# Seams between the stages of a fused eight-core decoder layer: an input load moved, normalisation work respread over the engines, output writes moved into the next pass

## Chip, cores and metric

The kernel is one SPMD program on all eight cores of one Trainium2 chip (two dies of four cores). The time is the device time of the slowest core, in microseconds (us). Engines: PE (TensorE, matmuls), DVE (VectorE), ACT (ScalarE), POOL (GpSimd, which also issues the weight loads here), SP (SyncE). An execution of all eight cores has a second, slower state, in which the cores of a die show a lower clock: in the changed kernel's run of 1408.84 us, cores 0 to 3 show 0.812 to 0.822 and the other four 0.989 or 0.990.

## The reference, cut to what matters

```python
def layer(h, p, ...):
    xn = rmsnorm(h); z = xn @ w_in                    # mixer A: short conv; mixer B: chunked gMLP
    ...
    h = h + m @ w_o
    up = rmsnorm(h) @ w_up                            # up-projection, then causal dwconv
    ...
    h = h + (jax.nn.gelu(fa) * fb) @ w_down           # down-projection
    gate = jax.nn.sigmoid(rmsnorm(h, g_ple) @ w_ple_gate)
    h = h + gate * (p @ w_ple)                        # per-layer embedding
y = rmsnorm(h, g_final)
```

There are 8 prompts of 2048 positions and 128 samples of one position, model width 1024, feed-forward width 2816. Each core takes one prompt and 16 samples.

## The kernel before

Activations lie channels first: 8 tiles of 128 channels, positions along the free axis. A core makes two passes of 1024 positions (pass 0 has its 16 samples too), each in three blocks of 384, 384 and 256 (272) positions. One pass is: first projection (v), conv stage (the head of it is seam A in pass 0 and seam D in pass 1), spatial stage, merge, output projection, up-projection (its start is seam B), down-projection, embedding stage (seam C in pass 0, seam E in pass 1). A list of operations per engine is built in program order, and semaphores are put in from the reads and writes, so **the order in which the Python code appends operations is the order in which each engine executes them**. That order is what the change is about. For example, on core 1 of the kernel before, POOL stood idle for 6.82 us, halved the embedding input (5.47 us) and issued the weight loads that stand behind it at 89.80 us.

A norm has four parts: squares on ACT, their sum over the 8 channel tiles on DVE or POOL, one matmul with ones that sums over the partitions (PE) and an Ln and an Exp on ACT, then 8 products. In the last stage of pass 1 (`self.pe`) PE sums the squares itself, with one small matmul for each tile into a held bank.

```python
class Norm:
    def _emit(self, k, b, late=False):
        ...
        if self.pe:                         # L444: square on ACT; L446: matmul with ones into the held bank
            if q == 0: self.bank[bi] = psR.get(hold=True)
            P.op("act", ... Square ...)
            P.op("pe", ... matmul(pt[:, 0:N], lhsT=ones[:], rhs=out, start=(q == 0), stop=(q == 7)) ...)
            return
        P.op("act", ... Square ...)                                         # L460
        ...
        P.op(self.eng, ... tensor_tensor(dst, acc, out, op=ALU.add) ...)     # L469, on POOL or DVE

    def rstd(self, b):
        self.flush(bi)
        pt, ptr = self.bank.get(bi) or psR.get()
        if bi in self.bank: psR.held.discard(ptr[1])        # the held bank goes back into rotation here
        else: group(pt[:, 0:N], [ones x ssb, ones x sqb])   # the statistics matmuls on PE
        P.op("act", ... Ln ...); P.op("act", ... Exp ...)   # L490, L491

    def to_xn(self, b, gi, spread=False):   # L501: 8 DVE products per block, input of the next projection
    def to_y(self, b, gi, parts, spread=False):  # L515: 8 DVE products in place, then stores
```

`bg` is a queue of such products: `spread=True` leaves them there, and `bg_run(n)` appends n of them between other work.

```python
def load_pT(p):                             # embedding input
    load(pT..., pt_d[p]..., eng="pool")
    P.op("pool", ... tensor_scalar(pT, pT, 0.5, op0=ALU.mult))              # L576
# called in pass 0 after setup_state(), in pass 1 after the first projection; that is, ahead of the conv stage

# start of the up-projection
for c in range(3):
    g_part(c, [b0])
    if c == 1: nrm.to_xn(b2, 1, True)
    else: bg_run(4)
for b in (b1, b2):
    for c in range(3):
        g_part(c, [b]); bg_run(4)
        ...

# embedding stage
fn = Norm(p, "pool", delay=2)
fn.pe = p == 1
for b in blocks:
    for i in range(8):
        fn.step()
        pG, pGr = psR.get(); pE, pEr = psR.get()
        proj(pG, ...); group(pE[:, 0:N], ...)                 # 8 + 2 matmuls
        ... tanh (ACT, L1015), gate (DVE, L1016), add (POOL or DVE, L1019) ...
        fn.add(i, b)
        bg_run(...)
        if bi == 0 and i == 0: nrm.to_xn(b1, 2, True)
        if bi == 0 and i == 7: nrm.to_xn(b2, 2, True)
        if bi > 0 and i == 1 and not (p == 0 and bi == 2): fn.to_y(blocks[bi - 1], 3, 2, True)
```

`psR` hands out the eight PSUM banks in rotation and skips held ones.

## Time and profile before

| kernel before | value |
|---|---|
| median of the four runs given first | 1260.41 us: two fast (1227.80, 1233.55), two slow (1287.27, 1289.82) |
| with the runs beside the changed kernel, 16 runs | median 1229.27 us |
| profiled run | span 1232.0 us on core 1 |

The median lies between two states. The spans of single cores in the profiled execution before show one more thing to note: the slowest core is 8.7 us above the median of the eight (1223.35, the mean of the fourth and fifth).

```profile
core 1: 1232.0 us, clock 0.977
...
core 7: 1218.1 us, clock 0.984
die 0 (median of its cores): 1225.0 us, clock 0.982
die 1 (median of its cores): 1222.3 us, clock 0.983
```

The dies agree, so the state is fast, and core 1 lost its excess by itself. One operation's statistics (count, then shortest, median and longest duration in ns) show a second thing, which isn't particular to core 1. It is the scaling of a tile of v on DVE:

```profile
L640 DVE TENSOR_SCALAR s_R<-s_R,s_rv x16: 475/478/5648, 79.6 to 707.7; 128x1024 bf16<-128x1024 bf16 x16
```

The same work took 0.48 us and, once, 5.65 us. The prediction takes the rest of the profile apart.

### The profile page before, as it was taken

To read this page: it belongs to the slowest core of one execution; us is meant where nothing else is said; L and a number is where in the kernel's file an instruction comes from. 1 tells how busy PE (TensorE), PEld (TensorE's weight loads), DVE (VectorE), ACT (ScalarE), POOL (GpSimd) and SP (SyncE) were. 2 spreads that over 40 slices of the span, in tenths; PEclk is the share of its full clock that TensorE was granted. 3 is DMA by queue.
4 is the path that set the end of the run, shared out by engine and by line. 5 is a ranking of instruction groups with operands and counts; after the bars stand their busy time and mean duration, and the time that the engine had idled before them with its cause. 6 is when DMAs were issued, how large, how long until landed. Compare 5 with 4: busy or idle time off the path is not lost.

```text
span 1232.0 us, 24272 instructions; the slowest of 8 cores (1218.1 to 1232.0 us)
## 1 busy us (share of the span) xinstructions
PE 1154.9 (94%) x7870; PEld 764.8 (62%) x7870; DVE 718.7 (58%) x1338; ACT 510.7 (41%) x1036; POOL 374.8 (30%) x411
## 2 busy tenths in 40 slices
PE   3898999999989999999889899999998999999975
PEld 2574666666656666666467566666665666666643
DVE  3346675222588999546663766522258899951266
ACT  3652232212446655343748133311134655541264
POOL 0140101222315343265560210122231534333241
PEclk9898999999999999999889899999999999999998
DMA  7737453333335332563349636333333533135303
GB/s 185 158 32 125 86 89 52 69 70 69 69 69 104 70 69 49 170 120 70 69 125 217 174 72 118 53 70 69 69 70 69 104 70 70 28 70 103 72 7 137
DMA packets 36234, 109.67 MB, mean 89 GB/s; under 512 B 10224, under 2 KB 10736, under 8 KB 35984
## 3 DMA queue, kind: packets, MB, share of 16 engines
q0 software_dynamic: 22016, 82.86, 37.6%
q1 hardware_dynamic: 14096, 25.27, 6.6%
q8 instruction: 67, 1.10, 0.3%
q14 instruction: 55, 0.45, 0.1%
HBM read 181.01 MB, written 9.95 MB: 155 GB/s over the span
## 4 chain that ended last, share of the span: by engine, by line
PE 79%; DVE 7%; ACT 6%; issue 4%; DMA 3%; POOL 1%; DVEq 0%; SPq 0%; POOLq 0%; ACTq 0%
PE pq L381 67%; PE pq L924 11%; DVE s_xn L501 3%; DMA s_ring<-win 2%; DMA s_h<-xt 1%; DVE s_h L515 1%; ACT L490 1%; ACT s_wide L613 1%; ACT s_rsb L490 1%; ACT s_R L606 1%; ACT L1015 1%; PE pq L679 1%; DVE s_R L640 1%; DVE s_wide L1016 1%; DVE s_h L819 1%
## 5 line engine op out<-in xcount | busy, mean ns | idle before, releaser
L381 PE MATMUL pq<-s_xn,s_ring 128*128 128x386 bf16 (+5 forms) x5184 | 801.6, 312 | 22.8 <-DVE s_xn L501 9.0
L381 PEld LDWEIGHTS pq<-s_xn,s_ring 128*128 128x128 bf16 x5184 | 503.7, 98 | 288.2 <-issue 39.8
L860 DVE SCALAR_TENSOR_TENSOR s_wide<-pq,s_cst,s_wide 128x384 f32<-128x384 f32 (+1 forms) x528 | 279.1, 568 | 31.0 <-ACT s_wide L852 2.7
L852 ACT ACTIVATE s_wide<-pq,s_cst 128x384 f32<-128x384 f32 (+1 forms) x264 | 138.3, 548 | 130.3 <-DVE s_wide L860 102.9
L867 POOL TENSOR_TENSOR s_R<-s_wide 128x1024 bf16<-128x1024 f32 x44 | 103.8, 2361 | 201.9 <-ACT s_wide L866 186.1
L924 PE MATMUL pq<-s_R,s_ring 128*128 128x384 bf16 (+2 forms) x1056 | 155.1, 309 | 0.0
L708 DVE SCALAR_TENSOR_TENSOR s_wide<-s_wide,pq 128x384 f32<-128x384 f32 (+2 forms) x96 | 49.2, 512 | 172.8 <-PE pq L381 172.8
L924 PEld LDWEIGHTS pq<-s_R,s_ring 128*128 128x128 bf16 x1056 | 103.2, 98 | 50.8
L381 PE MATMUL pq<-s_R,s_ring 128*128 128x384 bf16 (+2 forms) x768 | 119.8, 309 | 0.0
L706 ACT ACTIVATE s_wide<-pq 128x384 f32<-128x384 f32 (+2 forms) x96 | 43.9, 458 | 176.8 <-PE pq L381 142.5
L469 POOL TENSOR_TENSOR s_ss<-s_ss,s_sq 128x384 f32<-128x384 f32 (+2 forms) x84 | 80.4, 962 | 90.5 <-ACT s_sq L460 85.6
L381 PEld LDWEIGHTS pq<-s_R,s_ring 128*128 128x128 bf16 x768 | 75.0, 98 | 37.0
L460 ACT ACTIVATE s_sq<-s_h 128x384 f32<-128x384 f32 (+2 forms) x102 | 48.9, 486 | 117.9 <-DVE s_h L930 67.7
L710 POOL TENSOR_TENSOR s_xn<-s_wide 128x384 bf16<-128x384 f32 (+2 forms) x48 | 43.7, 911 | 166.3 <-DVE s_wide L708 166.3
L501 DVE SCALAR_TENSOR_TENSOR s_xn<-s_h,s_cst,s_rsb 128x384 bf16<-128x384 f32 (+2 forms) x120 | 74.2, 662 | 34.1 <-ACT s_rsb L491 33.9
L381 PE MATMUL pq<-s_ring,s_xn 128*128 128x256 bf16 (+1 forms) x544 | 69.3, 288 | 18.7 <-DMA s_ring<-win 12.5
L381 PEld LDWEIGHTS pq<-s_ring,s_xn 128*128 128x128 bf16 (+1 forms) x544 | 55.3, 102 | 32.7 <-issue 23.7
L930 DVE TENSOR_TENSOR s_h<-pq,s_h 128x384 f32<-128x384 f32 (+2 forms) x48 | 23.2, 510 | 85.5 <-PE pq L924 85.5
L654 ACT ACTIVATE s_wide<-s_wide,s_cst 128x384 f32<-128x384 f32 (+1 forms) x48 | 27.8, 579 | 104.8 <-DVE s_wide L652 104.8
L344 POOL DMA_DIRECT2D s_ring<-win x56 | 30.2, 545 | 80.8 <-DMA s_h<-xt 30.0
L656 DVE SCALAR_TENSOR_TENSOR s_wide<-s_wide,s_cst 128x384 f32<-128x384 f32 (+1 forms) x48 | 30.4, 633 | 38.3 <-ACT s_wide L654 38.3
L866 ACT ACTIVATE s_wide<-s_wide 128x1024 f32<-128x1024 f32 x44 | 46.9, 1067 | 0.9 <-DVE s_wide L860 0.9
(102 smaller groups left out, 729.6 us busy)
## 6 DMA issues: line engine op xcount, KB each, us to landing
s_ring<-win POOLq DMA_DIRECT2D x56, 512.0 KB, 8.6
s_ring<-wup POOLq DMA_DIRECT2D x44, 512.0 KB, 7.1
s_ring<-wdn POOLq DMA_DIRECT2D x16, 704.0 KB, 7.3
yt<-s_h SPq DMA_DIRECT2D x8, 768.0 KB, 3.5
s_ring<-woa POOLq DMA_DIRECT2D x8, 512.0 KB, 8.4
s_ring<-wob POOLq DMA_DIRECT2D x8, 512.0 KB, 10.1
s_ring<-wo POOLq DMA_DIRECT2D x8, 512.0 KB, 9.0
s_ring<-wg POOLq DMA_DIRECT2D x8, 512.0 KB, 6.5
```

Of the source, the lines that this page charges most:

```text
L381: P.op("pe", lambda e, l=l, r=r, q=q: e.matmul(out, lhsT=l, rhs=r, start=(q == 0), stop=(q == n - 1)), reads=list(reads) + list(rd), write ...
L460: P.op("act", lambda e: e.activation(out=out, in_=src, func=AF.Square), reads=rd, writes=[w])
L469: P.op(self.eng, lambda e: e.tensor_tensor(out=dst, in0=acc, in1=out, op=ALU.add), reads=[sr, w], writes=[dw])
L501: P.op("dve", lambda e: e.scalar_tensor_tensor(out=dst, in0=src, scalar=gcol(gi, k), in1=r[:, 0:N], op0=ALU.mult, op1=ALU.mult), reads=rd ...
L706: P.op("act", lambda e, tt=tt, pg=pg: e.activation(out=tt[:, 0:N], in_=pg[:, 0:N], func=AF.Tanh, scale=0.5), reads=[pgr], writes=ttr)
L708: P.op("dve", lambda e, tt=tt, py=py: e.scalar_tensor_tensor(out=tt[:, 0:N], in0=tt[:, 0:N], scalar=1.0, in1=py[:, 0:N], op0=ALU.add, op1= ...
L710: P.op("pool", lambda e: e.tensor_tensor(out=xns[1 - p][:, i, c0 + 2:c0 + 2 + N], in0=ta[:, 0:N], in1=tb[:, 0:N], op=ALU.add), reads=tar + ...
L852: P.op("act", lambda e, acc=acc, pt=pt, cc=cc, c0=c0, n=n: e.activation(out=acc[:, c0:c0 + n], in_=pt[:, 2:2 + n], func=AF.Copy, scale=wcf ...
L860: P.op("dve", lambda e, acc=acc, pt=pt, cc=cc, c0=c0, n=n, tap=tap: e.scalar_tensor_tensor(out=acc[:, c0:c0 + n], in0=pt[:, tap:tap + n], ...
L866: P.op("act", lambda e: e.activation(out=aa[:, 0:1024], in_=aa[:, 0:1024], func=AF.Gelu_apprx_tanh), reads=aar, writes=aar)
L867: P.op("pool", lambda e: e.tensor_tensor(out=act[:, c, 0:1024], in0=aa[:, 0:1024], in1=bb[:, 0:1024], op=ALU.mult), reads=aar + bbr, write ...
L924: P.op("pe", lambda e, c=c: e.matmul(pD[:, 0:N], lhsT=wd[:, c, :], rhs=act[:, c, c0:c0 + N], start=(c == 0), stop=(c == 21)), reads=wdr + ...
```

## The change

Its intent is to close the seams between the stages, without touching the matmuls. It has five parts, numbered as the prediction numbers them.

1. The embedding input is loaded and halved at the start of the down-projection. (Its buffer is then free during the up-projection and serves with the sums' buffer as two more accumulator pairs there.)
2. At the start of the up-projection, the eight products of the third block become an ACT scaling and a POOL multiply.
3. From down-projection to embedding: the sums go from POOL to DVE, the products of block 0 and half of block 1 are spread into the last units of the down-projection, and block 2's statistics come before the first tanh.
4. The output of pass 0 leaves the embedding stage: the statistics and the eight products of block 0 move into the first projection of pass 1. Those of blocks 1 and 2 were there already. Now all three statistics stand together, and the 24 products are spread.
5. In the embedding stage of pass 1 the sum-of-squares matmul lags three groups behind instead of two, and half of POOL's adds go to DVE.

```diff
@@ part 1
-                load_pT(0)
-            if p == 1:
-                load_pT(1)
+            load_pT(p)                      # start of the down-projection
+        upR = Rot(wideR.items + [(pT ... as F32), (ss[:, 0:1024] ...)])
-                    cs["acc"][c] = (wideR.get(), wideR.get())
+                    cs["acc"][c] = (upR.get(), upR.get())
@@ part 2
+                    if pool:
+                        t, tr = sqR.get()
+                        P.op("act", ... activation(out=t, in_=src, func=AF.Copy, scale=gcol(gi, k)) ...)
+                        P.op("pool", ... tensor_tensor(out=dst, in0=t, in1=r, op=ALU.mult) ...)
+                        return
             for c in range(3):
                 g_part(c, [b0])
+                bg_run(4)
                 if c == 1:
-                    nrm.to_xn(b2, 1, True)
-                else:
-                    bg_run(4)
+                    bg_flush(("xn", p, 1))
+                    nrm.to_xn(b2, 1, True, True)
@@ part 3
-            nrm = Norm(p, "pool")
+            nrm = Norm(p, "dve")
-                if p == 0 and b["idx"] == 0:
-                    anrm.to_xn(nb[1], 0)
-                if b["idx"] == 1:
-                    nrm.to_xn(b0, 2)
+                    bg_run(4)
+                    if i == 6 and b["idx"] == 0 and p == 0:
+                        anrm.to_xn(nb[1], 0, True)
+                    if i == 6 and b["idx"]:
+                        nrm.to_xn(blocks[b["idx"] - 1], 2, True)
+                    if bi == 0 and i < 2:
+                        tanhs.append(gate)
+                        if i == 1:
+                            nrm.to_xn(b2, 2, True)
+                            for f in tanhs:
+                                f()
+                    else:
+                        gate()
-                    if bi == 0 and i == 0:
-                        nrm.to_xn(b1, 2, True)
-                    if bi == 0 and i == 7:
-                        nrm.to_xn(b2, 2, True)
@@ part 4
-                    if bi > 0 and i == 1 and not (p == 0 and bi == 2):
+                    if p == 1 and bi > 0 and i == 1:
                         fn.to_y(blocks[bi - 1], 3, 2, True)
+                        if hf == 0 and bl == 1:                 # first projection of pass 1
+                            for b in blocks_of(0):
+                                fn.to_y(b, 3, 2, True)
+                        bg_run(8)
+                bg_run(24)
+                for b in blocks:
+                    load_h(1, b, 2)
@@ part 5
-            fn = Norm(p, "pool", delay=2)
+            fn = Norm(p, "pool", delay=2 + p)
-                    onpool = (i % 2 == 0) if p == 0 else bi < 2
+                        onpool = (p == 0 or bi < 2) and i % 2 == 0
```

Cut here: buffers that move to make room (one norm's sums into the state buffer, the last gain row into the squares' buffer), one v tile scaled later, half as many spread products after each group in the second and third block of the up-projection (`bg_run(2)` instead of `bg_run(4)`), and an option that lets output products run on POOL, which no call uses.

## The prediction

> **What bounds the kernel now.** I read the page of the slowest core (core 1) first, then the medians of the dies, then the waits of TensorE (PE), then stretches around each wait, then single instructions in them.
>
> ```profile
> span 1232.0 us, 24272 instructions; the slowest of 8 cores (1218.1 to 1232.0 us)
> PE 1154.9 (94%) x7870; PEld 764.8 (62%) x7870; DVE 718.7 (58%) x1338; ACT 510.7 (41%) x1036; POOL 374.8 (30%) x411
> ...
> PEclk9898999999999999999889899999999999999998
> ```
>
> PE is the bound, 94% busy; no other engine passes 58%. No matmul is added or removed, so the change can win only PE's idle 77.1 us (1232.0 - 1154.9) and what PE loses at a reduced clock. That bounds the gain: some 20 us of the idle time are start-up and the tail after the last matmul, which the change hardly touches.
>
> Who PE waits for (us, times, longest):
>
> ```profile
> PE pq L446 <- ACT s_wide L444: 21.3, 19, 4.4
> PE pq L381 <- DMA s_ring<-win: 18.6, 4, 8.3
> PE pq L381 <- DVE s_xn L501: 14.4, 22, 3.7
> PE pq L381 <- DVE s_wide L1016: 6.3, 5, 2.2
> PE pq L381 <- DVE s_wide L652: 3.3, 1, 3.3
> PE pq L381 <- DVE s_R L664: 1.5, 2, 1.3
> ```
>
> These are the sum-of-squares matmuls of the final norm, weights, normalised activations that are not there yet, and banks not yet emptied. Where they lie, as stretches (columns: PE, PE load, DVE, ACT, POOL busy; PE clock; DMA share; GB/s):
>
> ```profile
> 80.00:108.00 28.00, 21.87 (x128) 13.05 (x126) 18.37 (x33) 5.13 (x11) 9.74 (x11) 0.82 0.88 119
> 345.00:367.00 22.00, 18.25 (x102) 10.31 (x100) 20.17 (x39) 8.62 (x19) 0.60 (x2) 0.92 0.50 96
> 585.00:634.00 49.00, 39.75 (x224) 22.87 (x223) 35.68 (x57) 29.07 (x53) 27.46 (x27) 0.86 0.35 87
> 684.00:703.00 19.00, 14.22 (x80) 8.26 (x79) 14.66 (x20) 3.72 (x8) 7.52 (x6) 0.82 0.54 140
> 930.00:952.00 22.00, 18.04 (x114) 10.64 (x112) 19.61 (x39) 9.42 (x22) 1.66 (x4) 1.00 0.50 96
> 1164.00:1232.00 68.00, 44.90 (x266) 25.80 (x263) 41.81 (x77) 39.21 (x71) 20.07 (x18) 0.89 0.20 70
> ```
>
> These six seams hold nearly everything. I count a seam's loss as idle time plus length times (1 - clock), an estimate and an upper one where idle and slow time overlap: A, head of the conv stage of pass 0: 6.1 + 5.0 = 11.1; B, start of the up-projection: 3.8 + 1.8 = 5.6 in pass 0 and 4.0 in pass 1; C, embedding stage of pass 0: 9.3 + 6.9 = 16.2; D, head of the conv stage of pass 1: 4.8 + 3.4 = 8.2; E, embedding stage of pass 1: 23.1 idle, of which about 8 after the last matmul, and 7.5 of clock.
>
> One pair shows the cause of D:
>
> ```profile
> 687.12 5.65 DVE L640 TENSOR_SCALAR s_R<-s_R,s_rv 128x1024 bf16<-128x1024 bf16 x1
> 687.13 5.36 POOL L576 TENSOR_SCALAR s_pT<-s_pT 128x2048 bf16<-128x2048 bf16 x1 [20.41 <-DMA s_pT<-pt]
> ...
> 693.38 1.48 PE L381 MATMUL pq<-s_xn,s_ring 128*128 128x386 bf16 x8 [3.26 <-DVE s_wide L652]
> ```
>
> L640 takes 0.48 us at its other places (683.1, for one); here it took 5.65, ending with POOL's halving of the embedding input, and PE then stood 3.26 us. POOL had waited 20.4 us for that input.
>
> [...] PE's clock falls to 0.86 and 0.82 exactly in the stretches with waits and is 1.00 between them; so a wait can cost more than itself. [...] The trace: 1.00 us for POOL's accumulation of 128x384 without neighbours, 0.56 for DVE's.
>
> **The change, part by part.** The gains are for a usual core; the median core's span is 1223.
>
> 1. The embedding input is loaded at the start of the down-projection, not ahead of the conv stage. In A it kept POOL until 89.7, and the weights for the next pair were issued at 89.8 and missed by PE twice (2.4 and 3.7 us). POOL now goes from the state set-up, done at 76.8, to those loads: 13 us earlier, over the whole 6.1. Core 1 gains up to 9, another core where the weights came nearly in time 2: I take 2 (and keep the rest for the slowest core). In D the 5.65 us block goes, and with it 3.3 + 1.3 us of waits and slow clock on core 1; others had less: 5. In the down-projection POOL and DVE have room: PE ran 44.6 of 45 us from 540 to 585, and banks hold more than 20 us of its work there. Sum 7.
>
> 2. B. Eight DVE products for the third block become an ACT scaling into a buffer (about 0.43 us each) and a POOL multiply (about 0.85). DVE is the backlog there (20.2 of 22 us busy), POOL idle (0.6). The wait on this block, 2.4 + 0.9 us, and the slow clock after it (1.8) go nearly whole; the wait for the second block, 0.3 + 4 x 0.37 = 1.8, stays, as its jobs are in the same place of DVE's order. The last POOL product comes about when PE needs it, so I take 3.3 per pass: 6.5. The two more accumulator pairs are worth nothing: the up-projection has no PE wait after its first 20 us.
>
> 3. C. Norm sums of the down-projection go from POOL to DVE (0.56 instead of 1.0 us, and POOL stops blocking DVE's two-input products, which took 1.35 instead of 0.61). The products of block 0 and four of block 1 are spread into the down-projection; block 2's statistics come before the first tanh; the output of block 0 leaves the stage. ACT's table loads in the stage fall from 7 to 1. DVE work from 24 x 0.5 + 12 x 0.6 + 24 x 0.9 + 8 x 0.9 = 48 us to 12 + 7 + 12 x 0.9 = 30, in a stage of about 36 us of PE work. But it is still front-loaded: in the first block 8 x 0.55 + 4 x 0.7 + 11 x 1.0 = 18 us against PE's 8 x 1.63 = 13. The 8 banks take up four groups; I leave 1.3 us of wait for block 2's sums and 3.5 spread over the start of the second block[...]: 16.2 - 5 = 11, taken as 10.
>
> 4. The output of pass 0 (24 DVE products, 12 us) is now all written in the first projection of pass 1, where DVE was busy 15.7 of 34 us with 16 such products already. Three statistics stand together: 2 table loads instead of 4. The reloads of h come later, but are used 230 us later. 0.
>
> 5. E. The lag of the sum-of-squares matmul goes from two to three groups: 3 x 1.63 = 4.9 us for tanh 0.48 + gate 0.55 + add 1.2 + square 0.52 and four handovers of about 0.15, 3.4 together; the old 3.3 was just too little, which is the 0.4 to 1.7 us seen at nearly every group. Half of POOL's adds (1.2) go to DVE (0.68); table loads 10 to 6. Waits before the tail: 3.7 + 0.7 in block 0, 8.8 in block 1, 3.7 in block 2, 16.9 in all, and 2 of clock. I leave 5 in block 0 (same front-load as C), 2 in block 1, where DVE's 13.6 us stand against PE's 14.3, and 4 in block 2, whose 11.5 us of DVE exceed PE's 9.6 before and after: 19 - 11 = 8. The tail stays or grows by 0.4.
>
> Sum: 7 + 6.5 + 10 + 0 + 8 = 31.5 us.
>
> **Rivals.** First, DVE takes the place of the waits removed: it gets the down-projection's sums (18 per pass, each behind an ACT square in its own order) and still runs 18 us of work against 13. For it: seam C's 35.7 of 49 us on DVE; against it: POOL no longer blocks it, and 16 output products are gone. Then C and E give 9 instead of 18, and the time in the fast state is 1208. Second, the loads collide: the late embedding load in the down-projection blocks POOL's weight loads, or 4.2 MB of output and 4.2 MB of h meet the weights of pass 1. For it: stretch 650 to 684 ran at 236 GB/s; against it: the next weights are needed 20 us later. It would give back 5 to 8 us: about 1205. Third, only waits count and the clock does not recover: 5 us less. Fourth, everything behaves: 38 us, 1190.
>
> **Time, range, chances.** Median core 1223 - 31.5 = 1191.5. Core 1 was 9 above it, about 7 of that in seam A, which goes; I keep 5 for the slowest: 1196.5, plus 1.5 for the difference between run (1233.55) and span, 1198, and one for what I overlook: 1199 in the fast state, against 1230.7 (the mean of the two fast runs, 1233.55 and 1227.8): 2.6% faster. With an error of about 9 us (the first two rivals), the 2% line of 1206 is 0.8 errors off: 0.78 faster, 0.20 same, 0.02 slower. The median on record for the kernel before mixes two fast runs with two slow ones (1287 and 1290, 4.7% more). All fast would be 1199, half and half 1226; I say 1212, range 1188 to 1248, the upper part of it for the slow state.
>
> **What would show it.** Step 1: the halving of the embedding input between 505 and 600, no DVE row-scale over 1 us, waits on weights after 80 near zero. Step 2: under 1 us for the third block. Step 3: one table load in the first embedding stage, PE over 34 of its first 39 us, clock 1.00. Step 5: waits of the sum-of-squares matmul from 21.3 to about 14 (7 of them at the start). Wrong if DVE's gate or products stand as releaser of PE for more than 6 us in either embedding stage, if the clock there stays under 0.95, or if new waits on weights appear in the down-projection.

## The result, and the profile after

| | before | after |
|---|---|---|
| median, all runs | 1229.27 us (16 runs) | 1197.48 us (10 runs) |
| fast runs | 1225.4 to 1233.6 | 1196.1 to 1197.8 |
| slow runs | 3 (1287.27, 1289.82, 1398.01) | 2 (1238.84, 1408.84) |
| profiled span, slowest core | 1232.0 | 1196.2 |
| median of the eight cores in the profiled run | 1223.35 | 1193.85 |

The ratio is 0.974, with a 95% interval from 0.9727 to 0.9752. Ratios here and below are the mean time of one kernel's fast runs over the mean of the other's fast runs of the same rounds, so they are not quite the ratio of the medians quoted. Every kernel that ran, here and below, gave correct results.

The page of the changed kernel, slowest core (core 6):

```profile
span 1196.2 us, 24282 instructions; the slowest of 8 cores (1192.2 to 1196.2 us)
PE 1139.4 (95%) x7870; PEld 760.1 (64%) x7870; DVE 721.2 (60%) x1366; ACT 499.6 (42%) x1040; POOL 346.3 (29%) x383
...
PEclk9899999999999999999999999999999999999997
```

PE's idle time fell from 77.1 to 56.8 us (1196.2 - 1139.4), and PE's busy time by 15.5 us with the same 7870 matmuls. That second part is clock, whose mean is 0.977 on core 1 before and 0.990 on core 6 after: of the slices marked 8 ahead of the last one in the kernel before (the 2nd, in the start-up; the 4th, seam A; the 20th and 21st, C; the 23rd, D) only the start-up's is left.

What PE waits for after (us, times, longest):

```profile
PE pq L383 <- DMA s_ring<-win: 14.4, 2, 10.2
PE pq L447 <- ACT s_wide L445: 12.2, 12, 4.3
PE pq L383 <- DVE s_xn L507: 7.7, 16, 3.7
PE pq L383 <- ACT s_rsb L491: 4.2, 2, 2.1
PE pq L383 <- ACT s_wide L1031: 4.0, 5, 1.4
PE pq L383 <- POOL s_ssb L470: 2.0, 2, 1.3
PE pq L383 <- DVE s_wide L1032: 1.7, 4, 1.1
```

(Line numbers have shifted: L383, L447, L507 and L1032 are the L381, L446, L501 and L1016 of before.) Three rows fell: sums of squares from 21.3 to 12.2, normalised activations from 14.4 to 7.7, gates from 6.3 to 1.7. The rows on the conv stage (s_wide L652 and s_R L664 of before) have gone. Three rows are new or larger: the statistics of the last norm, s_rsb, 4.2; the tanh, L1031, 4.0; POOL's sums, s_ssb, 2.0 instead of 0.4. The two waits on weights now both lie in the first 40 us, the start-up.

The six stretches once more, cut at the same matmuls as those of the prediction (columns: PE, PE load, DVE, ACT, POOL busy; PE clock; DMA share; GB/s). They are A, B, C, D, B of pass 1, and E with the tail:

```profile
81.10:99.30 18.20, 18.20 (x127) 12.05 (x125) 12.93 (x28) 4.51 (x10) 1.99 (x5) 1.00 1.05 138
336.40:353.80 17.40, 15.97 (x102) 9.53 (x100) 15.67 (x29) 11.74 (x27) 6.92 (x9) 1.00 0.73 121
573.70:613.70 40.00, 35.06 (x223) 20.73 (x222) 29.61 (x48) 18.25 (x42) 24.04 (x23) 1.00 0.32 53
663.80:674.90 11.10, 11.10 (x81) 7.54 (x79) 8.14 (x17) 2.73 (x6) 1.77 (x4) 1.00 1.01 298
902.00:920.90 18.90, 17.27 (x113) 10.68 (x112) 16.19 (x29) 12.53 (x30) 7.61 (x11) 1.00 0.65 113
1133.00:1196.20 63.20, 43.85 (x265) 26.42 (x263) 42.58 (x83) 32.89 (x64) 9.04 (x8) 0.87 0.20 74
```

The lengths were 28, 22, 49, 19, 22 and 68 us on core 1 of before. So the stretches shrank by 9.8, 4.6, 9.0, 7.9, 3.1 and 4.8 us. The sum, 39.2, is a little more than the span gained (35.8), because this core's start-up waited 1.9 us longer on weights (14.4 us in its first 40, against 12.5) and its down-projection has the new 2.0. These are the slowest cores, and A was unusually long on core 1: on the mean of the eight cores it shrank by 4.8 us (table further below). A and D have no idle time left. In the first five the clock is 1.00, also in C, where PE is still idle for 4.9 of 40 us, but in waits of 1.1 us at most.

The embedding input is now halved in the down-projection. The first line is from the trace of POOL; the second has the durations of the v scaling (shortest, median, longest in ns):

```profile
510.91 5.47 POOL L591 TENSOR_SCALAR s_pT<-s_pT 128x2080 bf16<-128x2080 bf16 x1 [11.94 <-DMA s_pT<-pt]
```

```profile
L654 DVE TENSOR_SCALAR s_R<-s_R,s_rv x16: 475/478/486, 80.6 to 695.2; 128x1024 bf16<-128x1024 bf16 x16
```

The longest scaling is 486 ns where it was 5648.

The new row s_rsb of the wait list is one place, twice. These are the trace of PE, then that of ACT, in seam E after the change:

```profile
1154.30 0.32 PE L447 MATMUL pq<-s_wide,s_ones 128*128 128x384 bf16 x1 [0.47 <-ACT s_wide L445]
1156.72 2.72 PE L383 MATMUL pq<-s_xn,s_ring 128*128 128x384 bf16 x8 [2.10 <-ACT s_rsb L491]
```

```profile
1154.70 1.28 ACT L491 ACT_TABLE_LOAD   x1 [0.55 <-PE pq L447]
1156.00 0.58 ACT L491 ACTIVATE s_rsb<-pq,s_epsT 128x384 f32<-128x384 f32 x1
```

At 1154.30 PE adds the last sum of squares of a block to the held bank. At that point in the code the bank goes back into rotation, and the next gate matmul is given just this bank. It must wait until ACT has switched its table (1.28 us, as long as the mean of the 37 table loads on core 1 before) and read the bank (0.58 us). PE starts at 1156.72, after 2.10 us. The eight matmuls that follow took 2.72 us; groups of eight before the wait took 1.46. So the wait was paid once as idle time and again as slow clock: the packed trace has the granted clock at 0.50 from 1156.20 to 1159.62. All eight cores have these two waits of 2.1 us. On seven of them the stage has two slow spells ahead of its last 3 us, of 3.4 or 6.8 us each, and each begins within one of the two waits or at most 1.0 us after it. On core 1 the same wait slowed nothing:

```profile
1153.97 1.46 PE L383 MATMUL pq<-s_xn,s_ring 128*128 128x384 bf16 x8 [2.10 <-ACT s_rsb L491]
```

So the length of the wait alone does not decide it.

### The profile page after: what moved, and what is told of

Same layout as the page of the kernel before. It is cut to its first block, busy times and chain, and to the rows that moved or that the text cites. A ratio compares the mean times of both kernels' runs of the same rounds, so it can differ in the third digit from the quotient of the medians.

```text
span 1196.2 us, 24282 instructions; the slowest of 8 cores (1192.2 to 1196.2 us)
## 1 busy us (share of the span) xinstructions
PE 1139.4 (95%) x7870; PEld 760.1 (64%) x7870; DVE 721.2 (60%) x1366; ACT 499.6 (42%) x1040; POOL 346.3 (29%) x383
## 4 chain that ended last, share of the span: by engine, by line
PE 84%; DVE 6%; ACT 3%; issue 3%; DMA 2%; POOL 1%; DVEq 0%; SPq 0%; ACTq 0%; POOLq 0%
PE pq L383 75%; PE pq L936 8%; DVE s_xn L507 3%; DMA s_h<-xt 1%; POOL s_sst L470 1%; ACT s_sq L461 1%; DMA s_ring<-win 1%; DVE s_h L942 1%; PE pq L693 1%; DVE s_h L830 1%; ACT s_rsb L491 1%; DVE s_wide L1032 1%; DVE s_h L530 0%; ACT L491 0%; ACT s_rsb L492 0%
## 5 line engine op out<-in xcount | busy, mean ns | idle before, releaser
L383 PE MATMUL pq<-s_xn,s_ring 128*128 128x386 bf16 (+5 forms) x5184 | 787.5, 309 | 11.6 <-ACT s_rsb L491 4.2
L383 PEld LDWEIGHTS pq<-s_xn,s_ring 128*128 128x128 bf16 x5184 | 499.5, 97 | 269.2 <-issue 18.9
L871 DVE SCALAR_TENSOR_TENSOR s_wide<-pq,s_cst,s_wide 128x384 f32<-128x384 f32 (+1 forms) x396 | 209.9, 568 | 22.3 <-ACT s_wide L863 1.1
L863 ACT ACTIVATE s_wide<-pq,s_cst 128x384 f32<-128x384 f32 (+1 forms) x198 | 103.6, 549 | 85.3 <-DVE s_wide L871 76.4
L383 PE MATMUL pq<-s_R,s_ring 128*128 128x384 bf16 (+2 forms) x768 | 119.8, 309 | 0.0
L878 POOL TENSOR_TENSOR s_R<-s_wide 128x1024 bf16<-128x1024 f32 x33 | 78.0, 2363 | 134.5 <-ACT s_wide L877 125.3
L383 PEld LDWEIGHTS pq<-s_R,s_ring 128*128 128x128 bf16 x768 | 75.0, 98 | 37.0
L383 PE MATMUL pq<-s_ring,s_xn 128*128 128x256 bf16 (+1 forms) x544 | 68.4, 286 | 20.4 <-DMA s_ring<-win 14.4
L507 DVE SCALAR_TENSOR_TENSOR s_xn<-s_h,s_cst,s_rsb 128x384 bf16<-128x384 f32 (+2 forms) x104 | 63.5, 655 | 31.3 <-ACT s_rsb L492 31.2
L383 PEld LDWEIGHTS pq<-s_ring,s_xn 128*128 128x128 bf16 (+1 forms) x544 | 54.7, 102 | 34.1 <-issue 25.7
L670 DVE SCALAR_TENSOR_TENSOR s_wide<-s_wide,s_cst 128x384 f32<-128x384 f32 (+1 forms) x48 | 27.5, 574 | 38.5 <-ACT s_wide L668 36.3
L470 POOL TENSOR_TENSOR s_ss<-s_ss,s_sq 128x384 f32<-128x384 f32 (+2 forms) x39 | 39.4, 1011 | 31.7 <-ACT s_sq L461 29.6
L470 DVE TENSOR_TENSOR s_ss<-s_ss,s_sq 128x384 f32<-128x384 f32 (+2 forms) x40 | 24.2, 606 | 30.4 <-ACT s_sq L461 29.2
```

The source lines that it names most:

```text
L383: P.op("pe", lambda e, l=l, r=r, q=q: e.matmul(out, lhsT=l, rhs=r, start=(q == 0), stop=(q == n - 1)), reads=list(reads) + list(rd), write ...
L470: P.op(self.eng, lambda e: e.tensor_tensor(out=dst, in0=acc, in1=out, op=ALU.add), reads=[sr, w], writes=[dw])
L507: P.op("dve", lambda e: e.scalar_tensor_tensor(out=dst, in0=src, scalar=gcol(gi, k), in1=r[:, 0:N], op0=ALU.mult, op1=ALU.mult), reads=rd ...
L863: P.op("act", lambda e, acc=acc, pt=pt, cc=cc, c0=c0, n=n: e.activation(out=acc[:, c0:c0 + n], in_=pt[:, 2:2 + n], func=AF.Copy, scale=wcf ...
L871: P.op("dve", lambda e, acc=acc, pt=pt, cc=cc, c0=c0, n=n, tap=tap: e.scalar_tensor_tensor(out=acc[:, c0:c0 + n], in0=pt[:, tap:tap + n], ...
L878: P.op("pool", lambda e: e.tensor_tensor(out=act[:, c, 0:1024], in0=aa[:, 0:1024], in1=bb[:, 0:1024], op=ALU.mult), reads=aar + bbr, write ...
```

## The experiments

**Theory** (the prediction's): the parts act in different places and nearly add up, with 7 us for part 1, 6.5 for part 2, 10 for part 3, nothing for part 4 and 8 for part 5. **Rival**: the ordering of the embedding stages is worth little by itself (DVE or the clock remains the limit there), and the gain comes from the other parts. The runs undo one part at a time (names beginning with a_), or do one thing alone on the kernel before (names beginning with b_). A ratio is turned into us against the change's 0.974 with 1229 us. The kernels ran on three chips, so both the ratio and the medians are given. For b_part1, a_no1, a_no2 and a_no3, which ran on one chip, the ratio rests on only three fast runs of the kernel before, and a difference there is known to some 3 us. Against the 2% line the record calls b_part1 and b_port "same" and a_no1 to a_no4 "unclear"; the losses are read from the intervals, which for a_no1 to a_no4 and a_rstd4 do not overlap that of the change.

### b_part1: only part 1, on the kernel before

```diff
-                load_pT(0)
-            if p == 1:
-                load_pT(1)
+            load_pT(p)                      # start of the down-projection
```

> The kernel before with only the embedding input's load and halving moved to the start of the down-projection. Theory (the parts act on separate seams and add up): the waits at the heads of the two conv stages go, as between the two traces (about 4.8 us in pass 0 and 5.7 us in pass 1 per core), and about 1.4 us come back in the down-projection of pass 0: 1219 to 1221 us in the fast state against about 1229. Rival (the halving blocks DVE and POOL wherever it stands): the loss moves along, 1226 us or more. In the trace, under the theory, no row-scale of DVE above 1 us and no wait for weights after the first 80 us.

Measured: 1217.3 us, ratio 0.9915 [0.9895, 0.9934], which is 10.4 us. The v scaling and the waits of PE on weights, from this run:

```profile
L640 DVE TENSOR_SCALAR s_R<-s_R,s_rv x16: 476/477/486, 79.8 to 692.3; 128x1024 bf16<-128x1024 bf16 x16
```

```profile
PE pq L381 <- DMA s_ring<-win: 8.5, 1, 8.5
```

A third of the whole gain is this move. The block on DVE is gone, and one wait on weights is left, the start-up's.

### a_no1: the change without part 1

```diff
+                load_pT(0)                  # pass 0, after setup_state()
+            if p == 1:
+                load_pT(1)                  # pass 1, after the first projection
-            load_pT(p)
-        upR = Rot(wideR.items + [...])
+        upR = wideR                         # the two extra accumulator pairs need this buffer
```

> The changed kernel with the embedding input loaded and halved ahead of the conv stages again, as before (so its tile is no accumulator any more, and the up-projection has its six accumulators). Theory (parts add up): 1205 to 1208 us against 1197 of the whole change, the loss lying at the heads of the conv stages. Rival (the other parts, above all the earlier statistics in the first projection of pass 1, already give the conv stage its slack): under 1201 us.

Measured: 1204.67 us (1202.2 to 1206.7), ratio 0.9812 [0.9788, 0.9836], so 8.8 us are lost. The spans of three cores in its profiled run:

```profile
core 0: 1192.0 us, clock 0.991
...
core 2: 1192.1 us, clock 0.993
...
core 4: 1205.2 us, clock 0.986
```

Without part 1 the fastest cores stay at 1192, like those of the change, and one core is 13 us behind. Its wait list has four waits on weights, 18.0 us, where the change has two. The median core loses only 2.6 us (1196.45 against 1193.85). So this part sets much of the slowest core's excess, which is what the metric reads. The run takes the extra accumulators away too, and can't tell what those alone are worth. The trace of before has no wait of PE there that they could remove.

### b_port: the halving taken away from POOL, the wait for the input kept

Part 1 removes two suspects at once: POOL standing until the input has landed, which holds back the weight loads that it issues, and POOL's 5.4 us instruction, which blocks DVE. Here the load stays where it was and POOL still waits for it, but then copies only two columns; ACT does the halving at the start of the down-projection.

```diff
             load(pT[:, :, 0:nc_], pt_d[p][:, :, :], "pT", res, eng="pool")
-            P.op("pool", ... tensor_scalar(out=pT, in0=pT, scalar1=0.5, op0=ALU.mult) ...)
+            P.op("pool", ... tensor_copy(out=dmy[:], in_=pT[:, 0, 0:2]), reads=res ...)
+            half_pT(p)                      # ACT, start of the down-projection
```

> The kernel before with the halving of the embedding input done by ACT at the start of the down-projection; POOL still waits for the input to land at its old place, but then only copies two columns of it. This keeps POOL's wait of up to 20 us and takes away its 5.4 us instruction beside DVE's row-scale. Theory (the block of DVE by that instruction is the larger cost): 1221 to 1224 us against 1229, the head of the conv stage of pass 1 free of waits. Rival (the late issue of weights behind POOL's wait is the cost): 1227 us or more.

Measured: 1219.58 us, ratio 0.9928 [0.9912, 0.9945], which is 8.8 us of b_part1's 10.4. From the trace of POOL in seam A (the bracket has the idle time before), and the statistics of the v scaling:

```profile
84.50 0.18 POOL L577 COPY s_dmy<-s_pT 128x2 bf16<-128x2 bf16 x1 [7.01 <-DMA s_pT<-pt]
...
85.53 0.54 POOL L345 DMA_DIRECT2D s_ring<-win  x1 [0.71 <-PE pq L382]
```

```profile
L646 DVE TENSOR_SCALAR s_R<-s_R,s_rv x16: 476/478/581, 79.7 to 693.9; 128x1024 bf16<-128x1024 bf16 x16
```

POOL still stands 7.0 us for the input, and still only reaches the weight loads at 85.5, but the long scaling is gone and most of the gain is there. So the wait for the landing is the small part (PE's remaining wait on weights in seam A is 1.9 us here, against 6.1 before), and POOL's long instruction is the large one. In seam A that instruction did two things, stretching a DVE operation and delaying the issue by 4.3 us (89.8 to 85.5), and this run does not divide them. In seam D the trace names DVE's operation as what PE waited for. The block itself is plain: in the kernel before, on all eight cores and in both passes, just one DVE operation beside the halving took 2.6 to 5.7 us (the v scaling in 11 of the 16 cases, another product of the conv stage in the rest), and in b_port no DVE operation there takes over 2.5.

### a_no2: the third block's products on DVE again

```diff
                 g_part(c, [b0])
-                bg_run(4)
                 if c == 1:
-                    bg_flush(("xn", p, 1))
-                    nrm.to_xn(b2, 1, True, True)
+                    nrm.to_xn(b2, 1, True)
+                else:
+                    bg_run(4)
...
-                    bg_run(2)               # second and third block
+                    bg_run(4)
```

> The changed kernel with the products of the third block at the start of the up-projection on DVE again and in their old places. Theory: both passes lose the 4.2 us that their seam gained between the two traces: 1204 to 1207 us, with the slow clock back after that wait. Rival (it was the spread of the jobs, or the sums, not the engine, and DVE now has room): 1200 us or less.

Measured: 1200.76 us, ratio 0.9787 [0.9765, 0.9809]; lost: 5.8 us by the ratio, 3.3 by the medians. Seam B of pass 0 in this run:

```profile
336.00:357.50 21.50, 18.03 (x102) 10.17 (x100) 19.67 (x39) 8.64 (x19) 0.39 (x1) 0.92 0.55 98
```

It is 4.1 us longer than in the change (17.4), with DVE busy 19.67 of 21.5 us and the clock at 0.92, as before. Seam B returns; the mechanism of step 2 stands, though this run puts back the engine and the order together and can't divide them. That the time moved less than two such seams is partly that the waits of the down-projection's start are shorter in this run: its list has no row on POOL's sums, where the change has 2.0 us. Why they vanish there stays open.

### a_no3: the seam from down-projection to embedding as before

```diff
-            nrm = Norm(p, "dve")
+            nrm = Norm(p, "pool")
-                    bg_run(4)
-                    if i == 6 and b["idx"] == 0 and p == 0:
-                        anrm.to_xn(nb[1], 0, True)
-                    if i == 6 and b["idx"]:
-                        nrm.to_xn(blocks[b["idx"] - 1], 2, True)
+                if p == 0 and b["idx"] == 0:
+                    anrm.to_xn(nb[1], 0)
+                if b["idx"] == 1:
+                    nrm.to_xn(b0, 2)
...
-                    if bi == 0 and i < 2: tanhs.append(gate) ... else: gate()
+                    gate()
+                    if bi == 0 and i == 0:
+                        nrm.to_xn(b1, 2, True)
+                    if bi == 0 and i == 7:
+                        nrm.to_xn(b2, 2, True)
```

> The changed kernel with the seam between down-projection and embedding stage as before: sums on POOL, products issued in one go, no gate held back. Theory: the 8.5 us of the embedding stage of pass 0 are lost, and some 2 to 4 of pass 1: 1207 to 1210 us, with clock below 0.95 in the embedding stage of pass 0. Rival (the move of the first output out of the stage did most of it): 1201 to 1203 us.

Measured: 1201.93 us, ratio 0.979 [0.9771, 0.9809]; lost: 6.1 us by the ratio, 4.4 by the medians. The matmuls of C and of E up to the last in this run, and then in the change:

```profile
571.30:614.00 42.70, 36.51 (x222) 21.65 (x221) 30.10 (x50) 25.51 (x49) 27.28 (x27) 0.92 0.29 50
1133.30:1193.00 59.70, 43.31 (x266) 25.91 (x263) 40.27 (x77) 38.23 (x69) 10.76 (x10) 0.94 0.16 54
```

```profile
573.70:613.60 39.90, 34.96 (x222) 20.65 (x221) 29.51 (x48) 18.15 (x42) 24.04 (x23) 1.00 0.32 53
1133.00:1188.90 55.90, 43.48 (x264) 26.33 (x263) 39.33 (x75) 32.00 (x62) 9.04 (x8) 0.92 0.16 56
```

This ordering, with the sums on DVE, is worth 2.8 us in C and 3.8 in E. On the mean of the eight cores 1.9 us of it are paid back in the down-projection of pass 0, which is shorter without part 3 (79.1 us against 81.0). The prediction had put all of C's gain on it, with the output's move, and none of E's. This is nearer to the rival.

### a_pool: the down-projection's sums on POOL again

```diff
-            nrm = Norm(p, "dve")
+            nrm = Norm(p, "pool")
```

> The changed kernel with the down-projection's sums of squares on POOL again, all orders left as changed. Theory of the prediction's third step (POOL is slower and blocks DVE's two-input products near the end of the stage): 1199 to 1201 us, with DVE products above 1 us at the end of the down-projection. Rival (the order of the statistics and gates was all that counted): within 1 us of 1197.

Measured: fast runs 1195.0 to 1195.7 us, ratio 0.973 [0.9708, 0.9751], one slow run. This is 1.2 us less than the change, so moving these sums to DVE was worth nothing and may have cost about 1 us. The row of 2.0 us on POOL's sums (s_ssb) is not in its list. The median core says more clearly that it cost something: over the fast runs it takes 1189.6 to 1190.0 us here and 1192.7 to 1194.2 in the change, while the kernel before has 1222.4 to 1222.7 on the three chips of the experiments (means of fast runs). The down-projection of pass 0 is 1.5 us shorter here. POOL's sums together with the late return of the bank (a_bank) were not run.

### a_no4: the output of pass 0 written in its old places

```diff
-                    if p == 1 and bi > 0 and i == 1:
+                    if bi > 0 and i == 1 and not (p == 0 and bi == 2):
                         fn.to_y(blocks[bi - 1], 3, 2, True)
...
+                        if hf == 0 and bl == 0:
+                            bg_flush(("y", 0)); load_h(1, b0, 2)
                         if hf == 0 and bl == 1:
-                            for b in blocks_of(0): fn.to_y(b, 3, 2, True)
-                        bg_run(8)
-                bg_run(24)
-                for b in blocks: load_h(1, b, 2)
+                            fn.to_y(blocks_of(0)[1], 3, 2); load_h(1, b1, 2)
+                        if hf == 1 and bl == 1:
+                            fn.to_y(blocks_of(0)[2], 3, 2); load_h(1, b2, 2)
```

> The changed kernel with the writing of pass 0's output in its old places: block 0 in the embedding stage, blocks 1 and 2 one by one in the first projection of pass 1. Theory (undoing the seam's own reordering cost only 2.3 us in the embedding stage of pass 0, of the 8.5 gained there, so the output's departure gave the other 6): 1202 to 1204 us, with table loads back in that stage. Rival (the move of the output is worth nothing by itself, as the prediction's fourth step has it): 1196 to 1199 us.

Measured: 1204.02 us, ratio 0.98 [0.9784, 0.9816]; lost: 7.4 us by the ratio, 6.5 by the medians. This is the largest loss but for part 1, where the prediction had 0 (it had counted the move's effect in step 3). Seam C of this run, the longest wait of PE in it, and POOL's work just before that wait ends:

```profile
571.90:619.00 47.10, 36.99 (x222) 21.61 (x221) 35.21 (x55) 21.83 (x45) 25.02 (x23) 0.93 0.42 83
```

```profile
PE pq L383 <- POOL s_ssb L470: 6.2, 1, 6.2
```

```profile
592.84 1.14 POOL L1037 TENSOR_TENSOR s_h<-s_wide,s_h 128x384 f32<-128x384 f32 x1 [1.32 <-DVE s_wide L1034]
593.93 1.32 POOL L470 TENSOR_TENSOR s_ss<-s_ss,s_sq 128x384 f32<-128x384 f32 x1
595.45 0.99 POOL L470 TENSOR_TENSOR s_ssb<-s_ss,s_sq 128x384 bf16<-128x384 f32 x1 [0.20 <-ACT s_sqb L461]
```

With the output in the stage, PE reaches the statistics matmul of block 0 while POOL is still adding that block's squares, and stands 6.2 us. In the kernel before, the matmul stood at the same place, and there was no such wait in seam C, because PE was late by its other waits: on the slowest core, counted from the first matmul of the stage, POOL's sum was done at 24.3 us and PE came at 25.2. Here the sum is done at 25.1 and PE was ready at 19.1. **So part 3 needs part 4**: the first lets PE arrive early, the second takes away what it would then wait for. The reverse does not hold. On the mean of the eight cores C takes 51.7 us before and 42.6 in the change, 50.0 with part 3 and without part 4, and 45.2 with part 4 and without part 3: part 3 without part 4 gains 1.7 of the 9.1, part 4 without part 3 gains 6.5.

### a_rstd4: only the statistics of block 0 back in the embedding stage, its products later

To divide a_no4 into the statistics (matmul, two table switches, Ln, Exp) and block 0's eight DVE products.

```diff
+                    if p == 0 and bi == 1 and i == 1:
+                        keep = list(bg); del bg[:]
+                        fn.to_y(b0, 3, 2, True)
+                        ykeep = list(bg); bg[:] = keep
...
+                            bg.extend(ykeep)              # its products in the first projection of pass 1
-                            for b in blocks_of(0):
+                            for b in blocks_of(0)[1:]:
```

> The changed kernel, but the statistics of pass 0's first output block (two matmuls, logarithm and exponential, two table switches) stand in the embedding stage of pass 0 as before, while its eight products stay in the next stage. With the whole output back in its old places the run took 1204 us. Theory (the table switches in front of the tanh are what the embedding stage paid): 1202 to 1204 us. Rival (DVE's eight products were the cost): 1197.5 to 1199 us, with one stall of about a microsecond at the switch.

Measured: 1201.14 us, ratio 0.9776 [0.9761, 0.9791], so 4.4 us are lost, 60% of a_no4's loss, with no product moved. Its seam C, and the wait:

```profile
571.40:615.90 44.50, 36.95 (x222) 21.95 (x221) 31.28 (x50) 23.08 (x48) 24.35 (x25) 0.92 0.27 47
```

```profile
PE pq L383 <- POOL s_ssb L470: 6.2, 1, 6.2
```

The same wait of 6.2 us and the same slow clock come from the statistics of one block of the three. ACT's table loads in the stage are 3 in both, 1 in the change.

### a_no5: lag of two groups and the adds on POOL again, in pass 1

```diff
-            fn = Norm(p, "pool", delay=2 + p)
+            fn = Norm(p, "pool", delay=2)
-                        onpool = (p == 0 or bi < 2) and i % 2 == 0
+                        onpool = (i % 2 == 0) if p == 0 else bi < 2
```

> The changed kernel with the sum-of-squares matmul of pass 1 two groups behind again instead of three, and all adds of blocks 0 and 1 of that stage on POOL again. Theory of the prediction (the lag is what the stage waits for): the stage loses most of its gain, 1201 us or more. Rival (the stage is now held by two table switches, each in front of a bank that the next matmul wants at once, and by DVE, so the lag matters little): 1197 to 1199 us.

Measured: 1197.07 us, ratio 0.9745 [0.9726, 0.9764]. Part 5, predicted at 8 us, is worth nothing. The waits in seam E of this run, and then of the change:

```profile
PE pq L447 <- ACT s_wide L445: 13.9, 15, 4.0
```

```profile
PE pq L447 <- ACT s_wide L445: 6.7, 9, 2.1
PE pq L383 <- ACT s_rsb L491: 4.2, 2, 2.1
PE pq L383 <- ACT s_wide L1031: 1.4, 1, 1.4
```

The longer lag did halve the waits on sums of squares, from 13.9 to 6.7. In their place stand the wait for the bank and one for a tanh, together 5.6. What is left of the difference, 1.6 us of idle time, is too little to show: the interval of this ratio is 2.3 us to either side. Over all eight cores, up to the last matmul of the stage, PE idles for 13.4 us here and 12.2 in the change, but 5.5 us of the stage lie at the slow clock here and 9.9 in the change. The lag won idle time and lost it to the clock.

### a_bank: the held bank goes back into rotation four requests later

```diff
                 if bi in self.bank:
-                    psR.held.discard(ptr[1])
+                    freed.append([4, ptr[1]])     # get() counts down and then gives it back
```

> The changed kernel, but the bank that held a block's sum of squares is kept out of the rotation for four more bank requests after its statistics are issued, so that the next projection does not want it before ACT has switched tables and read it. Theory (pass 1's embedding stage gave less than predicted because of that wait, 2 x 2.1 us on every core): 1192 to 1194 us, and the wait of PE for ACT's logarithm gone. Rival (ACT is held up by the switch in any case and PE waits for the next tanh instead): 1196 us or more.

Measured: fast runs 1192.9 to 1193.9 us, ratio 0.9714 [0.9698, 0.973], one slow run. This is 4.1 us less than the change by the medians, 3.2 by the ratio. The waits of seam E and the stretch of its matmuls:

```profile
PE pq L454 <- ACT s_wide L452: 11.2, 11, 2.5
PE pq L390 <- ACT s_wide L1038: 1.4, 1, 1.4
```

```profile
1132.00:1185.10 53.10, 40.34 (x266) 25.03 (x263) 39.39 (x75) 31.83 (x62) 9.05 (x8) 0.99 0.17 60
```

The row s_rsb is gone, and yet the waits sum to about the same (12.8 with the activations' 0.2, against 12.3): the sums of squares came to be waited for instead. But the clock is 0.99 instead of 0.92, PE is busy for 40.3 instead of 43.5 us, and the stretch is 2.8 us shorter. So the gain is in the clock: the same amount of idle time, divided otherwise, slowed the matmuls less. These lines are of the slowest core of each kernel. Over all eight cores, from the first to the last matmul of the stage on each, the means are: length 56.8 us in the change and 53.7 here, PE idle 12.2 and 12.3, clock 0.91 and 0.98. Which property of the waits decides it (their length, or two close together, or when they fall) is not settled by this run, whose longest is 2.5 us. The interval of the ratio touches that of the change (0.9727), but no fast run of the one lies among those of the other.

### best1 and best2: toward a version that beats both kernels

best1 is a_bank with a lag of four groups in pass 1; best2 is best1 with two statistics of the next pass read later in the down-projection, against the 2.0 us on POOL's sums.

```diff
@@ best1 (on a_bank)
-            fn = Norm(p, "pool", delay=2 + p)
+            fn = Norm(p, "pool", delay=2 + 2 * p)
@@ best2 (on best1)
-                    elif i == 3:
+                    if p == 0 and b is b0 and i == 4:
                         anrm.to_xn(nb[0], 0)
                         stage_x(nb[1])
                         norm_x(2)
-                    elif i == 4:
+                    if p == 0 and b is b0 and i == 5:
                         anrm.to_xn(nb[2], 0)
                         norm_x(1)
```

> The variant with the accumulator bank given back late (1193.4 us), and in pass 1 a lag of four groups for the sum-of-squares matmul. Theory (two waits of 1.9 and 2.7 us behind the table switches remain there, as the square stands behind the switch in ACT's order, and one group more of lag covers them): 1189 to 1191 us. Rival (DVE or ACT is full there, or the tail grows by a square and a matmul): 1193 us or more.

> As the run with four groups of lag, and the statistics for pass 1's first and third block are read one group later in the down-projection of pass 0. Theory (the change made the sums late there, 0.4 us of wait before and up to 2.0 after): 1 to 1.5 us faster than the run with four groups of lag. Rival (the wait lies within what the slowest core hides): no difference beyond 0.5 us.

Measured: best1 1192.92 us, ratio 0.9708 [0.9694, 0.9723]; best2 1196.64 us, ratio 0.9738 [0.9724, 0.9753]. best1 is the fastest kernel, 2.9% faster than before and clear of the change's interval. It isn't told apart from a_bank: the fourth group of lag is worth half a microsecond or nothing (on the mean of the eight cores it takes 1.8 us of idle time from E, but the clock there falls from 0.98 to 0.95). best2 is a miss. Its list shows one wait on POOL's sums in the down-projection:

```profile
PE pq L390 <- POOL s_ssb L477: 3.8, 1, 3.8
```

Moving the statistics moved the next sums too (`norm_x` sits behind them), and one wait of 3.8 us took the place of two short ones. The traces place the loss there: on the mean of the eight cores the down-projection of pass 0 is 4.3 us longer than in best1 and C 0.8 shorter, and no other stretch moves by more than 0.1.

## Why the prediction was right or wrong

**The whole.** The changed kernel is faster, as held most likely. In the fast state 1199 was predicted and 1197 measured. The 31.5 us for a usual core became 29.5 (1223.35 - 1193.85), and the slowest core's excess fell from 8.7 to 2.4 us where 5 was kept: two errors that nearly cancel. That is luck in part, and so is the sum: step 4, taken as 0, brought about 7 us, and step 5's 8 did not come. The 1212 is 14.5 above the median, because it assumed a mixture of states (its "half and half" of 1199 and 4.7% more is 1227, not 1226); only 2 of 10 runs of the changed kernel were slow, so the median fell in the fast state.

**The sum.** By the ratios, undoing the parts one at a time loses 8.8, 5.8, 6.1, 7.4 and 0.6 us, together 28.7 of 32. By the medians it is 7.2, 3.3, 4.4, 6.5 and -0.4, together 21. The first sum says that the parts nearly add up; the second says that they overlap. The kernel before speaks for the second: its median core takes 1222.4, 1222.5 and 1222.7 us on the three chips (fast runs), so the chips hardly differ. Against the predicted 7, 6.5, 10, 0 and 8 both say the same: step 3 too large, step 4 far too small, step 5 empty.

The traces say where they overlap. These are the mean lengths, rounded, in us over the eight cores of the profiled run, from the first matmul of a stretch to the first of the next. Columns: conv and spatial stages (with seam A or D at their head), output and up-projection (with seam B), down-projection, embedding stage (C; E up to the last matmul).

| run | A | B | down, pass 0 | C | D | B, pass 1 | E |
|---|---|---|---|---|---|---|---|
| before | 125.8 | 191.8 | 79.4 | 51.7 | 123.3 | 189.0 | 61.8 |
| b_part1 | 121.1 | 191.5 | 79.3 | 51.6 | 118.9 | 188.2 | 61.7 |
| change | 121.1 | 187.6 | 81.0 | 42.6 | 117.6 | 184.9 | 56.8 |
| a_no1 | 125.2 | 187.6 | 80.2 | 42.6 | 118.5 | 184.9 | 56.3 |
| a_no2 | 121.1 | 191.6 | 79.5 | 42.3 | 117.6 | 187.5 | 55.4 |
| a_no3 | 121.1 | 187.6 | 79.1 | 45.2 | 117.6 | 184.9 | 60.6 |
| a_no4 | 121.1 | 187.6 | 81.0 | 50.0 | 117.7 | 184.8 | 57.3 |
| a_no5 | 121.1 | 187.6 | 80.7 | 42.6 | 117.6 | 184.8 | 57.5 |
| a_pool | 121.1 | 187.6 | 79.5 | 42.2 | 117.6 | 184.9 | 55.7 |
| a_bank | 121.1 | 187.7 | 80.5 | 42.6 | 117.6 | 184.9 | 53.7 |

Each part acts in its own seams. They overlap in D, where part 1 alone gains 4.4 us and the other parts without it 4.8, together 5.7. And the down-projection of pass 0, which the change makes 1.6 us longer, is shorter again in most runs that undo a part. The prediction had no term for that. E differs by up to 1.4 us between the change and runs that don't touch it.

**Step 1** was right in mechanism and too small: 8.8 to 10.4 us instead of 7. The mis-sized term is seam A. I summed what PE lost in each seam over all matmuls of the eight cores (start to start, less the time that the same matmul takes in undisturbed stretches): from before to b_part1, A fell by 4.8 us on the mean core, where 2 was taken, and D by 4.4, where 5 was. b_port shows POOL's instruction, not the wait for the landing, to be the larger cause, and a_no1 shows that the slowest core depends on it. One thing the sum had not foreseen: in a_no1, which lacks part 1, D is only 0.9 us longer than in the change and A 4.1, so within the whole change part 1 is worth its time in A.

**Step 2** held: seam B shrank by 4.6 and 3.1 us on the slowest cores and by 4.2 and 4.0 on the mean of the eight, against twice 3.3, and a_no2 brings the seam back. (The two waits that the step names, 3.3 and 1.8 us, are more than the 3.8 us of idle time on its own line: the trace has 2.2 for the third block and 0.6 for the second.) The third block's products are out of the wait; what remains of activations' waits in seam B is 1.1 us, all of it before matmuls of 386 columns, which are the second block's (the third has 272 or 256 and two more).

**Step 3** gave seam C 9.0 us by the trace, against 10 (16.2 less what was left, rounded down), so the size of the seam was right. Its working was not. It rested on DVE's work falling from 48 to 30 us, though the prediction's own line has DVE busy for only 35.7 of 49 us; and a_rstd4 gives DVE little more to do in the seam (31.3 us against 29.5) and loses over 4 us there. The sums on DVE, to which the step gave a place, are worth less than nothing (a_pool), and the ordering is worth 2.8 us in C (a_no3). The rest of C is the output's leaving, which the prediction counted here without a number of its own.

**Step 4** is where the attribution failed. The 0 looked only at where the output went, not at what it left. The step's own sentence on table loads (two instead of four) was right, but the statistics matmul had been overlooked: as soon as PE is early, it waits 6.2 us for POOL's sums (a_no4, a_rstd4). Moving the output is worth 6.5 to 7.4 us, more than half of it by the statistics and not by DVE's products.

**Step 5** failed outright. The sum 4.9 against 3.4 us for the lag was worked out rightly, and the waits on sums of squares did fall (13.9 to 6.7). But the bank that the sum was held in came next in rotation, behind a table switch, and at the head of the stage PE met a tanh that stood behind another switch of table (1.4 us) (a_no5). The term that failed is the count of waits left over: it looked at each row by itself and not at what PE asks for next once a row is shorter. The prediction named as a general rival that only waits count and the clock does not recover; in this seam that is what happened (0.89 before and 0.87 after, with the tail), and a_bank shows that part of it can be had. The prediction's reading that the clock falls exactly in the stretches with waits was also too simple: its own stretch 930 to 952 idles 4.0 us at 1.00. What seam E gained, 4.8 us with the tail, comes for the most part from step 3's ordering (a_no3: 3.8).

**The rivals.** The first (DVE takes the place of the waits) did not come in C and E: DVE's gate and products together release 2.1 us of PE's waits in C (1.7 and 0.4). What it says of the sums given to DVE has a smaller truth: a_pool does better without them. The second (colliding loads) did not come: no wait on weights after 40 us. The third came in E alone.

**What would show it.** Of the tests written down, these passed: the halving at 511; no v scaling over 1 us; no wait on weights after 80; one table load in seam C; clock 1.00 there, with PE busy 35.0 of 39.9 us; the sum-of-squares row at 12.2 where about 14 was said; and under 1 us for the third block in seam B, where no wait is left. One passed in part: the clock in E is 0.87 with the tail (0.92 without), so the test "under 0.95" fired for E and rightly pointed at step 5.

## What to carry to other kernels

When the bound engine is 94% busy, look at each seam for the operation that *issues* or *releases* something while standing behind an unrelated wait or in an unrelated place of program order: a load's follow-up work on the engine that issues other loads, a statistics matmul whose input another engine is late with, a bank given back before its reader has read it. A change that makes the bound engine arrive earlier uncovers the next wait, so list what it will meet there before giving the step its microseconds. And read the clock beside the waits: 4.9 us of idle time spread over 40 cost only themselves here (seam C, clock 1.00), while in another seam one of 2.10 us was followed by matmuls at half the clock (0.50) on seven of eight cores, and dividing the same waits otherwise won 3 us.
